# A streaming trunk layer: input-projection blocks in another order, decay matrices masked on VectorE in pairs, and head norms joined 120 matmuls later

## The chip, the cores and the metric

The kernel runs on one core of a Trainium2 chip. The time is device time in microseconds (us); the figure of a kernel is the median over its runs. TensorE (PE) multiplies matrices, VectorE (DVE), ScalarE (ACT) and GpSimd (POOL) do elementwise work, SyncE (SP) starts DMAs.

## The reference

One layer of a hybrid encoder for 256 prompt rows and 64 rows of a running stream, with one set of fp32 weights. A combined input projection feeds two groups of channels: 8 convolution groups (gate, causal convolution of width 31, group norm, swish) and 8 heads of a gated delta rule. Then come one output projection and a feed-forward network. Cut to what matters here:

```python
h = rmsnorm(x, g_pre_mix)
p = h @ w_in            # columns: conv values, conv gates, q, k, v, z, beta and decay inputs
# convolution groups
u = h_val * sigmoid(h_gate)
u = causal_dwconv(u, buf, w_dw, b_dw)              # 31 taps
a_out = silu(group_norm(u))
# heads
qkv = silu(causal_dwconv(qkv, buf, w_sc))          # 4 taps
G = cumsum(g)                                      # g: log decay of each row and head
decay = exp(where(incl, G[i] - G[j], -inf))        # lower triangle, for each head and chunk
m = where(strict, (k * beta) @ k.T * decay, 0);  tmat = inverse(m + eye)
o = ...                                            # chunked recurrence with tmat and decay
o = o * rsqrt(mean(o * o) + EPS) * onorm_g         # head norm
b_out = o * silu(z)
x = x + rmsnorm(concat(a_out, b_out) @ w_out, g_post_mix)
# feed-forward: w_up, convolution of width 3, silu(gate) * up, w_down
```

## The kernel before

All 320 rows are the moving side of each matmul, 128x320. A weight block of 128 output channels and 2048 inputs comes as two DMA halves of 128x1024. ScalarE rounds a half to `whi` (L182), VectorE subtracts to get the rest, `wlo` (L183), and a block takes 48 matmuls: for each of its 16 slices `whi` by the high part of the rows, `whi` by their low part (L198, L199), and `wlo` by the high part (L202). There are three buffers for a split half. These 48 are called dense matmuls below; the blocks follow each other on TensorE without any other order than the program's.

The input projection has 56 such blocks. `PLAN`, a list of steps, sets their order: `c0` is the gate block and the value block of convolution 0, `h0` the k, q and v blocks of head 0, `z0` the block of head 0's output gate, and `g` starts the decay matrices of all heads. `FIRST` names four blocks that are multiplied ahead of the list, while the rows are still being split; `in_block` hands them out of `ready` when the list comes to them.

The work that is not dense is written as jobs, Python generators. After each 20 dense matmuls (`GAP`) the jobs that are due are moved on by one step, and a `yield` with a number of matmuls (`LAG_...`) says how much later the next step may be issued. A step issues a few small matmuls and the elementwise work behind them. As each engine runs its instructions in order, a small matmul whose input is late holds up all dense matmuls behind it. The jobs that matter here:

- `gates`: from `baT` (L378) through the log decay `gt` (L412) to six small matmuls into `psg` (L423), exponentials on ScalarE, and then five rounds: VectorE spreads the decays (`rg`, L441), TensorE sums them (`psd`, L444), ScalarE takes the exponential (`eg`, L445), GpSimd multiplies by a triangle of ones and stores the piece of a head's decay matrix `E` (L448).
- `conv_block` and `conv_tail`: after the value block come one tap on ScalarE (L473) and 30 taps on VectorE (`cvt`, L475). 400 matmuls later (`LAG_CONV`) TensorE transposes the result (`pt_c`, L484), and the group norm follows, from `bst` (L486) to `un` (L495).
- `gdn_tail` and `pair`: two heads make a pair. Its triangular inverse is found by levels of small matmuls (`pz`, `px`, `py`, L685 to L693, joined on VectorE in `wtp`, L694 and L695), then the recurrence runs (`vn`, `po`, L740 and L742). The head norm scales the result `ot` on ScalarE (L805), and after `LAG_NORM` matmuls TensorE transposes it (`pt_o`, L814).

ScalarE holds one set of function tables at a time; where a function of another set follows, the program has an `ACT_TABLE_LOAD` of its own ahead of it.

## Time and profile before

| what | value |
|---|---|
| median of 3 runs | 1543.32 us (1542.33 to 1543.33) |
| the profiled execution's own time | 1543.88 us |
| its span in the trace | 1542.1 us |
| TensorE busy | 1513.1 us, 98% of the span |
| VectorE, ScalarE, GpSimd busy | 1006.5, 728.3 and 332.5 us |
| TensorE idle in the stretch from 40 to 560 us | 18.1 us |

The profiled execution is one run, 0.56 us above the median; some 1.8 us of it lie outside the span. Busy time of TensorE counts a matmul from its start to its modelled end, also where the clock is low, so that a slow stretch is hidden in it.

### The profile page before, as it was taken

What the parts mean: (1) busy time and instruction counts of PE and PEld (TensorE: products, weight loads), DVE (VectorE), ACT (ScalarE), POOL (GpSimd) and SP (SyncE); (2) the same over time, 40 slices, a digit from 0 to 9 for tenths busy, and PEclk for the clock granted to TensorE, in tenths of its full rate; (3) what the DMA queues carried; (4) which work ended last, traced back from release to release, by engine and by line L of the source; (5) the groups of instructions that cost most, each with busy time, mean ns of one, the idle gap of its engine ahead of it and who ended that gap; (6) DMA issues with size and microseconds to landing.
All of it is one profiled execution on the core that took longest, in us unless ns stands there. A gap on an engine that the chain in (4) does not pass through costs nothing.

```text
span 1542.1 us, 26538 instructions
## 1 busy us (share of the span) xinstructions
PE 1513.1 (98%) x10249; PEld 1489.1 (97%) x10249; DVE 1006.5 (65%) x1828; ACT 728.3 (47%) x1203; POOL 332.5 (22%) x501
## 2 busy tenths in 40 slices
PE   9989999989999999999999999999999999999998
PEld 8979999989899998899999999999999999999997
DVE  6789969586898468756534666545566545566554
ACT  7655464545545465544434444433444333444453
POOL 0354424153211000323101222101222101232101
PEclk9999999999999999999999999999999999999999
DMA  8434444353444563344445444445444345444443
GB/s 295 143 95 145 126 122 142 105 153 113 109 132 127 154 232 113 115 153 145 132 150 167 148 151 150 129 151 172 151 151 151 127 150 168 153 147 153 131 150 115
DMA packets 95991, 224.31 MB, mean 145 GB/s; under 512 B 18424, under 2 KB 37112, under 8 KB 95736
## 3 DMA queue, kind: packets, MB, share of 16 engines
q1 hardware_dynamic: 95720, 222.57, 46.4%
q8 instruction: 81, 1.33, 0.4%
q14 instruction: 46, 0.38, 0.1%
q10 hardware_dynamic: 144, 0.03, 0.0%
HBM read 215.45 MB, written 7.12 MB: 144 GB/s over the span
## 4 chain that ended last, share of the span: by engine, by line
PE 80%; DVE 12%; POOL 3%; ACT 2%; issue 2%; DMA 1%; SPq 0%; DVEq 0%; ACTq 0%; POOLq 0%
PE psu L202 13%; PE psu L198 13%; PE psu L199 13%; PE psdn L198 7%; PE psdn L199 7%; PE psdn L202 7%; DVE wlo L183 4%; DVE cvt L475 3%; PE psq L202 2%; PE psq L198 2%; PE psq L199 2%; PE psm L202 1%; PE psm L198 1%; PE psm L199 1%; PE ps_first L352 1%
## 5 line engine op out<-in xcount | busy, mean ns | idle before, releaser
L182 ACT CAST whi<-w 128x1024 fp32r<-128x1024 f32 (+2 forms) x432 | 411.3, 954 | 516.7 <-PE psu L199 170.7
L183 DVE TENSOR_TENSOR wlo<-w,whi 128x1024 fp32r<-128x1024 f32 (+2 forms) x432 | 477.1, 1105 | 198.1 <-ACT whi L182 111.4
L198 PE MATMUL psu<-hi,whi 128*128 128x320 f32 x1344 | 397.5, 309 | 2.9 <-DVE fbuf L1014 2.9
L199 PE MATMUL psu<-lo,whi 128*128 128x320 f32 x1344 | 397.5, 309 | 0.0
L198 PEld LDWEIGHTS psu<-hi,whi 128*128 128x128 f32 x1344 | 252.6, 188 | 3.4 <-DVE fbuf L1014 3.4
L199 PEld LDWEIGHTS psu<-lo,whi 128*128 128x128 f32 x1344 | 252.7, 188 | 0.0
L1015 POOL COPY nffn<-fbuf 128x2 f32<-128x2 f32 x88 | 101.4, 1152 | 599.5 <-DVE fbuf L1013 598.9
L202 PE MATMUL psu<-hi,wlo 128*128 128x320 f32 x1344 | 225.5, 310 | 0.0
L199 PE MATMUL psdn<-gl,whi 128*128 128x320 f32 x704 | 208.9, 309 | 0.0
L198 PE MATMUL psdn<-gh,whi 128*128 128x320 f32 x704 | 208.8, 310 | 0.0
L202 PEld LDWEIGHTS psu<-hi,wlo 128*128 128x128 f32 x1344 | 204.9, 189 | 0.0
L1013 DVE TENSOR_TENSOR fbuf<-psu,rb 128x256 f32<-128x256 f32 x88 | 37.4, 425 | 177.3 <-PE psu L202 174.8
L475 DVE SCALAR_TENSOR_TENSOR cvt<-ub,par,cvt 128x350 f32<-128x350 f32 x240 | 139.8, 596 | 2.7 <-ACT cvt L473 0.2
L198 PEld LDWEIGHTS psdn<-gh,whi 128*128 128x128 f32 x704 | 132.1, 188 | 0.8 <-ACT gh L206 0.8
L199 PEld LDWEIGHTS psdn<-gl,whi 128*128 128x128 f32 x704 | 132.1, 188 | 0.3
L202 PE MATMUL psdn<-gh,wlo 128*128 128x320 f32 x704 | 124.0, 309 | 0.0
L202 PEld LDWEIGHTS psdn<-gh,wlo 128*128 128x128 f32 x704 | 108.5, 188 | 0.0
L198 PE MATMUL psq<-hh,whi 128*128 128x320 f32 x352 | 106.1, 315 | 0.8 <-DVE baT L379 0.8
L199 PE MATMUL psq<-hl,whi 128*128 128x320 f32 x352 | 104.9, 311 | 0.0
L198 PEld LDWEIGHTS psq<-hh,whi 128*128 128x128 f32 x352 | 66.9, 190 | 1.1 <-ACT whi L182 1.0
L199 PEld LDWEIGHTS psq<-hl,whi 128*128 128x128 f32 x352 | 66.9, 190 | 0.0
L1057 DVE TENSOR_TENSOR y<-y,psdn 128x320 f32<-128x320 f32 x48 | 23.4, 488 | 63.9 <-PE psdn L202 63.9
(314 smaller groups left out, 2369.1 us busy)
## 6 DMA issues: line engine op xcount, KB each, us to landing
w<-in_w_up SPq DMA_DIRECT2D x176, 512.0 KB, 3.6
w<-in_w_in SPq DMA_DIRECT2D x88, 512.0 KB, 3.5
w<-in_w_down SPq DMA_DIRECT2D x64, 384.0 KB, 3.0
w<-in_w_down SPq DMA_DIRECT2D x64, 320.0 KB, 2.7
w<-in_w_out SPq DMA_DIRECT2D x32, 384.0 KB, 3.1
w<-in_w_out SPq DMA_DIRECT2D x8, 512.0 KB, 3.7
w<-in_w_first SPq DMA_DIRECT2D x6, 512.0 KB, 5.4
wtp<-wsp SPq DMA_DIRECT2D x4, 640.0 KB, 5.2
```

Of the source, the lines that this page charges most:

```text
L182: S.copy(hi[:, 0:width], w[:, 0:width])
L183: V.tensor_tensor(lo[:, 0:width], w[:, 0:width], hi[:, 0:width].bitcast(F32), ALU.subtract)
L198: tick(PE.matmul(ps, wh, xh, start=(k0 + j == 0), stop=False))
L199: tick(PE.matmul(ps, wh, xl, start=False, stop=False))
L202: tick(PE.matmul(ps, lo[:, j * P:(j + 1) * P], xh, start=False, stop=(final and k0 + j == nk - 1)))
L352: tick(PE.matmul(ps, w, xh, start=(k == 0 and wt is hi), stop=(k == KB - 1 and wt is lo)))
L475: V.scalar_tensor_tensor(cvt, ub[:, t:t + 350], pv("w_dw", b * 31 + t), cvt, ALU.mult, ALU.add)
L1013: V.tensor_tensor(buf[:, 2:258], psu[:, 0:TP], rb2[:, 0:TP], ALU.mult)
L1015: G.tensor_copy(nffn[:, b, 0, :], buf[:, 256:258])
L1057: V.tensor_tensor(y[:, n, :], y[:, n, :], psd[:, 0:T], ALU.add)
```

## The change

Five edits, in the order of the code:

- `FIRST` names the output-gate blocks of heads 0 and 1 (40 and 41) in place of the gate and value block of convolution 0. `PLAN` begins with them, starts `g` next, and then alternates heads and convolutions.
- `LAG_NORM` goes from 60 to 120.
- The decay matrices of two heads share one tile, `E2`. The triangle is multiplied on VectorE, for two heads in one instruction, 12 in all, in place of 24 on GpSimd. Tiles of the output projection and the feed-forward network that used the old buffers take halves of the new ones.
- A convolution that stands two before in the list is finished between the gate block and the value block of a `conv_block`, and no longer ahead of both.
- At heads 2, 4 and 6 the first block of the head is multiplied ahead of what was forced there, and the pair before the last is moved on only until its head norm is scaled (`free`), and no longer finished.

```diff
-LAG_NORM = 60
+LAG_NORM = 120
-PLAN = "c0 g h0 h1 c1 z0 c2 z1 h2 h3 z2 z3 c3 h4 h5 c4 z4 h6 h7 c5 z5 c6 z6 z7 c7"
+PLAN = "z0 z1 g h0 h1 c0 z2 h2 c1 h3 z3 c2 h4 c3 z4 h5 c4 h6 c5 z5 h7 c6 z6 z7 c7"
-FIRST = (8, 0, 24, 16)
+FIRST = (40, 41, 24, 16)
     def split_mix(i, x):
-        b_hi[i] = act.tile([P, T], F32R, tag=f"bh{i}", name=f"bh{i}")
+        if i < 8:
+            b_hi[i] = act.tile([P, T], F32R, tag=f"bh{i}", name=f"bh{i}")
+        elif i % 2 == 0:
+            both = act.tile([P, 2, T], F32R, tag=f"bp{i // 2 - 4}", name=f"bp{i // 2 - 4}")
+            b_hi[i:i + 2] = both[:, 0, :], both[:, 1, :]
...
-        E = [act.tile([P, T], F32, tag=f"bh{8 + h}", name=f"E{h}") for h in range(NH)]
+        E2 = [act.tile([P, 2, T], F32, tag=f"bp{i}", name=f"E{i}") for i in range(NH // 2)]
+        E = [E2[h // 2][:, h % 2, :] for h in range(NH)]
...
             S.activation(eg, psd, AF.Exp)
-            for j in range(w):
-                m = cv("tri") if c < 2 else cv("tri2")[:, (j % 2) * n:(j % 2 + 1) * n]
-                G.tensor_tensor(E[h0 + j][:, c * P:c * P + n], eg[:, j * n:(j + 1) * n], m, ALU.mult)
+            for j in range(w // 2):
+                if c < 2:
+                    m = cv("tri").unsqueeze(1).to_broadcast((P, 2, n))
+                else:
+                    m = cv("tri2").rearrange("p (b i) -> p b i", b=2)
+                V.tensor_tensor(E2[h0 // 2 + j][:, :, c * P:c * P + n],
+                                eg[:, 2 * j * n:2 * (j + 1) * n].rearrange("p (b i) -> p b i", b=2), m, ALU.mult)
...
         psv = in_block(b, "psv")
+        if b > 1:
+            finish(convs[b - 2])
...
             S.activation(ot[:, a, :], ot[:, a, :], AF.Identity, scale=t1[:, a:a + 1])
+        st["free"] = True
         yield LAG_NORM, 0, 2
...
     def z_block(h):
-        psz = ps_p.tile([P, 512], F32, tag="p", name="psz")
-        block_matmul(psz[:, 0:T], ins["w_in"][40 + h], hx, (8, 8))
+        psz = in_block(40 + h, "psz")
...
         if kind == "c":
-            if i > 1:
-                finish(convs[i - 2])
             convs[i] = start(conv_tail(i, conv_block(i)), LAG_CONV, 0, 1)
...
             if i % NS == 0:
-                if i // NS > 1:
-                    finish(pairs[i // NS - 2])
+                if i:
+                    ready[24 + i] = in_block(24 + i, "psq")
+                while i // NS > 1 and "free" not in sts[i // NS - 2]:
+                    advance(pairs[i // NS - 2])
                 st = {}
+                sts.append(st)
                 pairs[i // NS] = start(pair(i // NS, st), 0)
```

How the change moves instructions, at three places. The first is ScalarE in the stretch where the decay matrices are made. Before, one table load (L426, for the exponentials) stands there, the five `eg` follow it, and the next load belongs to the sigmoid of an output gate, `zT`:

```order
L463 ACT_TABLE_LOAD
L463 ACTIVATE sg<-sg 128x320
L182 CAST whi<-w 128x1024
L426 ACT_TABLE_LOAD
L426 ACTIVATE eG<-psg 128x24
...
L445 ACTIVATE eg<-psd 128x512 x2
L182 CAST whi<-w 128x1024
L445 ACTIVATE eg<-psd 128x512
L473 ACTIVATE cvt<-ub_589,par 128x350
L827 ACT_TABLE_LOAD
```

After, on ScalarE from the second `eg` of the five on, with the short convolution's `vts` and the gate `sg` of convolution 0 between them:

```order
L550 ACT_TABLE_LOAD
L550 ACTIVATE vts<-cq 128x64
L450 ACT_TABLE_LOAD
L450 ACTIVATE eg<-psd 128x512
L182 CAST whi<-w 128x1024
L472 ACT_TABLE_LOAD
L472 ACTIVATE sg<-sg 128x320
L182 CAST whi<-w 128x1024
L450 ACT_TABLE_LOAD
L450 ACTIVATE eg<-psd 128x512
```

The exponentials have moved in among other functions, so that tables are loaded between them; the whole program has 22 such loads before and 29 after.

The second place is VectorE where the first convolution is joined. Before, the last taps of convolution 0 (input `ub_588`) alternate with those of convolution 1 (`ub_589`), right in front of the group norm's `BN_STATS`, which reads what TensorE has transposed:

```order
L475 SCALAR_TENSOR_TENSOR cvt<-ub_588,par,cvt 128x350
L475 SCALAR_TENSOR_TENSOR cvt<-ub_589,par,cvt 128x350
L475 SCALAR_TENSOR_TENSOR cvt<-ub_588,par,cvt 128x350
L589 TENSOR_SCALAR tq_1279<-ssq_598 128x2
L475 SCALAR_TENSOR_TENSOR cvt<-ub_589,par,cvt 128x350
L590 TENSOR_SCALAR tq_1279<-ssq_598 128x2
L475 SCALAR_TENSOR_TENSOR cvt<-ub_589,par,cvt 128x350
L486 BN_STATS bst<-pt_c 128x6 x2
```

After, on VectorE, the last tap of convolution 0 (line numbers have moved by 11), then what is left of a pair's inverse, 14 taps of convolution 1 and splits of weights (cut here), and the join:

```order
L658 TENSOR_TENSOR tmp<-wi,dn 40x72
L486 SCALAR_TENSOR_TENSOR cvt<-ub_588,par,cvt 128x350
L471 TENSOR_TENSOR sg<-psgate,rb 128x320
L660 TENSOR_REDUCE wi<-tmp 40x2x6
L183 TENSOR_TENSOR wlo<-w,whi 128x1024
...
L486 SCALAR_TENSOR_TENSOR cvt<-ub_589,par,cvt 128x350
L548 SCALAR_TENSOR_TENSOR cq<-qb_594,par,cq 128x323
L183 TENSOR_TENSOR wlo<-w,whi 128x1024
L497 BN_STATS bst<-pt_c 128x6 x2
```

The taps of one convolution no longer alternate with the next one's, and 41 rows stand between the last of them and the group norm, 8 of them `wlo`. Counted so for convolutions 0 to 7, VectorE has 0, 5, 1, 6, 4, 0, 8 and 13 `wlo` between the last tap and the join before, and 8, 7, 5, 8, 3, 6, 6 and 11 after.

The third place is TensorE between the recurrence of heads 2 and 3 (pair 1) and the transposes of their norm. Before, the last `po`, one block's first 40 dense matmuls (cut here), `pt_o`:

```order
L740 MATMUL po<-vn,kd 128x128 x2
L742 MATMUL po<-vn,at 128x128 x2
L198 MATMUL psq<-hh_90,whi 128x320
...
L199 MATMUL psq<-hl_121,whi 128x320
L814 MATMUL pt_o<-cst,ot 128x128 x6
L202 MATMUL psq<-hh_98,wlo 128x320
```

After, on TensorE, with 120 dense matmuls between the two:

```order
L751 MATMUL po<-vn,kd 128x128 x2
L753 MATMUL po<-vn,at 128x128 x2
L202 MATMUL psgate<-hh_94,wlo 128x320
...
L202 MATMUL psq<-hh_101,wlo 128x320
L826 MATMUL pt_o<-cst,ot 128x128 x6
L202 MATMUL psq<-hh_102,wlo 128x320
```

For pairs 0 to 3 the numbers of dense matmuls between the last `po` and `pt_o` are 60, 40, 60 and 80 before, and 120 for each after. From the second part of the output projection on, VectorE, ScalarE and GpSimd have the same instructions in the same order as before.

## Rows read from the trace of the kernel before

**Rows 1.** Page, part 1: busy us (share of the span) and instructions by engine.

```profile
PE 1513.1 (98%) x10249; PEld 1489.1 (97%) x10249; DVE 1006.5 (65%) x1828; ACT 728.3 (47%) x1203; POOL 332.5 (22%) x501
```

**Rows 2.** Stretches: length, busy us of each engine, granted clock, DMA share, GB/s.

```profile
40.00:560.00 520.00, 501.89 (x3442) 491.64 (x3441) 409.79 (x840) 273.34 (x574) 154.94 (x224) 0.98 0.44 134
560.00:1542.00 982.00, 972.54 (x6564) 961.67 (x6563) 570.19 (x951) 427.51 (x588) 174.07 (x269) 1.00 0.47 145
```

**Rows 3.** What TensorE waited for: us in total, times, longest us.

```profile
PE pt_o L814 <- ACT ot L805: 7.3, 2, 4.2
PE pt_c L484 <- DVE cvt L475: 4.7, 2, 4.2
...
PE pz L685 <- DVE wtp L695: 2.1, 1, 2.1
...
PE psq L198 <- DVE baT L379: 0.8, 1, 0.8
PE psg L423 <- DVE gt L412: 0.7, 1, 0.7
```

**Rows 4.** Stretches before 560 us with a granted clock of 0.50; columns as in Rows 2.

```profile
84.10:87.40 3.30, 3.30 (x9) 2.27 (x9) 2.36 (x4) 0.60 (x1) 1.86 (x3) 0.50 0.44 127
108.00:111.30 3.30, 2.92 (x12) 2.92 (x13) 2.68 (x13) 0.27 (x2) 2.52 (x6) 0.50 0.21 86
268.40:275.10 6.70, 6.70 (x28) 6.70 (x28) 6.02 (x12) 1.79 (x4) 0.19 (x1) 0.50 0.34 86
319.60:322.90 3.30, 2.64 (x11) 2.64 (x12) 1.67 (x5) 2.46 (x6) 0.00 (x0) 0.50 0.47 156
415.20:418.50 3.30, 3.02 (x13) 3.03 (x14) 2.11 (x3) 2.10 (x3) 0.86 (x1) 0.50 0.00 0
```

**Rows 5.** Timeline of TensorE around the norms of pairs 1 and 2: start, us.

```profile
309.53 0.61 PE L742 MATMUL po<-vn,at 128*128 128x128 f32 x4
...
320.26 1.54 PE L814 MATMUL pt_o<-cst,ot 128*128 128x128 f32 x6 [4.25 <-ACT ot L805]
...
403.06 0.61 PE L742 MATMUL po<-vn,at 128*128 128x128 f32 x4
...
415.48 1.54 PE L814 MATMUL pt_o<-cst,ot 128*128 128x128 f32 x6 [3.01 <-ACT ot L805]
```

**Rows 6.** Timeline of TensorE in a dense stretch: eight matmuls, and the one behind them.

```profile
42.54 1.34 PE L202 MATMUL psq<-hh,wlo 128*128 128x320 f32 x8
43.72 0.31 PE L198 MATMUL psq<-hh,whi 128*128 128x320 f32 x1
```

**Rows 7.** Timeline of VectorE at the first convolution's join and in pair 1's levels.

```profile
105.77 2.55 DVE L475 SCALAR_TENSOR_TENSOR cvt<-ub,par,cvt 128x350 f32<-128x350 f32 x5
...
263.13 3.67 DVE L475 SCALAR_TENSOR_TENSOR cvt<-ub,par,cvt 128x350 f32<-128x350 f32 x6
```

**Rows 8.** Groups by line, 34 to 560 us: busy, mean ns; idle before, releaser.

```profile
L183 DVE TENSOR_TENSOR wlo<-w,whi 128x1024 fp32r<-128x1024 f32 (+1 forms) x123 | 142.9, 1162 | 54.4 <-ACT whi L182 31.6 <-PE psm L202 12.5 <-PE psq L202 4.1
...
L182 ACT CAST whi<-w 128x1024 fp32r<-128x1024 f32 (+1 forms) x124 | 122.8, 994 | 83.4 <-PE psm L199 27.9 <-PE psq L199 19.4 <-PE psgate L199 10.9
...
L448 POOL TENSOR_TENSOR E<-eg,cst 128x128 f32<-128x128 f32 (+1 forms) x24 | 15.4, 672 | 4.3 <-ACT eg L445 4.3
```

**Rows 9.** Timeline of VectorE, two of the five spreads of the decays.

```profile
85.72 0.69 DVE L441 TENSOR_TENSOR rg<-cst,gt 128x512 f32<-128x512 f32 x1 [0.91 <-PE psd L444]
...
91.11 0.95 DVE L441 TENSOR_TENSOR rg<-cst,gt 128x512 f32<-128x512 f32 x1
```

**Rows 10.** Timeline of ScalarE around a table load, and at one `eg`.

```profile
59.11 0.24 ACT L539 ACTIVATE vts<-cq 128x64 f32<-128x64 f32 x1
59.36 1.28 ACT L389 ACT_TABLE_LOAD   x1
60.66 0.22 ACT L389 ACTIVATE beta<-ba 128x24 f32<-128x24 f32 x1
...
88.78 0.60 ACT L445 ACTIVATE eg<-psd 128x512 f32<-128x512 f32 x1 [2.47 <-POOL E L448]
```

More of the change, by code (lines that the diff above doesn't have):

```diff
@@ L840, in trunk_kernel @@
     plan = PLAN.split()
-    tails, convs, pairs = {}, {}, {}
+    tails, convs, pairs, sts = {}, {}, {}, []
     for step in plan:
@@ L1028, in trunk_kernel @@
     for q in range(NQ):
-        gh = [act.tile([P, T], F32R, tag=f"bh{j}", name=f"gh{j}") for j in range(QB)]
+        gh = [act.tile([P, T], F32R, tag=f"bh{j}", name=f"gh{j}") for j in range(8)]
+        for i in range(2):
+            both = act.tile([P, 2, T], F32R, tag=f"bp{i}", name=f"gp{i}")
+            gh += [both[:, 0, :], both[:, 1, :]]
         gl = [act.tile([P, T], F32R, tag=f"bl{j}", name=f"gl{j}") for j in range(QB)]
```

## The prediction, made before the result was known

> **What bounds the kernel now.** I read the page's first part before anything else. TensorE is busy for 98% of the span, VectorE for 65%, ScalarE for 47% and GpSimd for 22% [rows 1]. The change adds no dense matmul and takes none away, so it can win only what TensorE loses, and it can lose wherever TensorE begins to wait. The next view is the two stretches: from 40 to 560 us (input projection and the first part of the output projection) TensorE is busy 501.89 of 520.00 us, and behind it 972.54 of 982.00 [rows 2]. The instructions of the second stretch are the same in both kernels, so only the 18.1 us of idle time in the first are in reach.
>
> The third view says what this idle time waited for: the transposes of two head norms 7.3 us, those of two convolutions 4.7, one level of an inverse 2.1, the gates' `baT` 0.8 and `gt` 0.7 [rows 3]. That is 15.6 us; 2.5 are left in small waits.
>
> The fourth view is the clock. Five stretches before 560 us show a granted clock of 0.50, the 1.2 GHz level in place of 2.4, with TensorE busy 18.58 us in all [rows 4]. At the full clock about half of that would do, so another 9.3 us are lost, which no list of waits shows. Four of the five stretches lie where TensorE had just stood still for 2 to 4 us (the norms at 320.26 and 415.48 [rows 5], the first convolution's join, the level). The fifth, at 84 us, follows the short wait for `gt` and six small matmuls. Waits and clock together make 27.4 us, which is the most that this change can win.
>
> A rule for the cost of a moved join: a dense matmul starts 0.147 us after the one before (eight from 42.54 to 43.72 [rows 6]), so 120 of them cover 17.7 us, 60 cover 8.8.
>
> **The change, part by part.**
>
> *Head norms.* Pair 1's last `po` starts at 309.53 and `pt_o` could start at 320.26: 10.7 us. Pair 2's chain takes from 403.06 to 415.48, 12.4 us [rows 5]. With 40 and 60 matmuls ahead they were 4.25 and 3.01 us late. After the change each pair has 120, 17.7 us, so both have some 5 us to spare, and no input of the chain is moved behind it. I take away the 7.3 us and half of the slow stretches that follow (2.64 and 3.02 us busy, 2.8 us): −10.1.
>
> *Convolution joins.* The stall of 4.2 us came where the last taps of convolution 0 alternate with those of convolution 1: five taps end at 108.32 [rows 7], and TensorE starts there. The other of the two, 0.5 us, was convolution 5's join. These are the joins with no split of weights between last tap and group norm (0 of both 0 and 5 in the counts by convolution). In the new order the least count is 3 and six of eight have 6 or more. TensorE needs each split within a half block's 24 matmuls, 3.5 us, so a tap that stands ahead of three splits which TensorE must have read before the join ends some 5 us or more before it. I take away 4.7 us and half of 2.92: −6.2. The bound: nothing gained, where VectorE runs late as a whole.
>
> *Pair 1's level.* Six taps in a row, 3.67 us from 263.13, stood ahead of `wtp` [rows 7]; TensorE waited 2.1 us and then ran 6.70 us at the lower clock. In the new order no `wtp` of this pair stands behind more than one tap. −2.1 − 3.35 = −5.5.
>
> *The gates.* The output gates of heads 0 and 1 stand ahead of them in place of convolution 0. One more VectorE operation stands ahead of `baT`, worth some 0.4 us, so that I take 1.2 in place of 0.8; the chain to `gt` meets about the same matmuls, and I take 1.0 in place of 0.7 and 0.3 for the first `psd`. The low clock at this place I leave as it is. Small waits grow from 2.5 to 3.1, since there are as many joins as before. Together +1.6; from −1.5, if all these go, to +4.
>
> *Masks.* 24 multiplications leave GpSimd, 15.4 us [rows 8], and 12 come to VectorE. The trace shows no such instruction. The nearest is the spread `rg` of 512 columns, 0.69 us with GpSimd idle and 0.95 beside the masks [rows 9]; half its columns is about 0.35 us, a quarter 0.2: eight and four of them make 3.6 us. Bounds are 0 (if what VectorE gets back from an idle GpSimd is as much: 0.26 us for each of several operations) and 12 × 0.95 = 11.4. VectorE is busy 409.79 of 520.00 us [rows 2], 79%, so 3.6 us more find room; TensorE pays only where a join is late, which the joins above carry. 0.
>
> *Table loads.* 7 more, 1.28 us each [rows 10], are 9.0 us on ScalarE, most of them among the five `eg`. In this stretch of some 21.5 us of dense matmuls I count for ScalarE 7 loads 9.0, 7 `whi` of 0.99 [rows 8] 7.0, five `eg` of 0.6 [rows 10] and, estimated, as much in small ones, less what overlaps, 5.5: 21.5 us. So it is just full there, with three buffers of split weights ahead. I take 0, since a load is issued ahead of its data, in time in which ScalarE waited (83.4 us ahead of `whi` in the whole stretch [rows 8]). The other end is 9.0, all of it.
>
> The trace shows the function ahead ending at 59.35, the load starting at 59.36 and ending at 60.64, and the next function starting at 60.66 [rows 10]: nothing drains on either side of it. The Trainium skill, page "ScalarE: Activation LUTs", section "What ACT_TABLE_LOAD costs", puts a switch at a 1283 ns load and a drain of about 1380 ns, 2.66 us together. The trace agrees with the load and shows no drain; by the page seven loads would be 18.6 us, and if all of it came to TensorE the forecast would lose its whole gain.
>
> *The other edits* add no instruction. A convolution's tail, forced between gate and value block, and a pair, forced behind the k block, get 48 dense matmuls more ahead of them, 7.1 us of cover; the pair is forced only as far as its scaled norm. Weight loads keep number and size and follow the order of the blocks on SP's queue, with DMA busy 44% [rows 2]; no split waits for them longer than before as long as that queue runs three buffers ahead. 0; without that cover they are the late joins that come next.
>
> *What comes late instead.* In the new VectorE order four taps stand right ahead of a `wtp` of pair 3, two thirds of the stack that cost pair 1 its stall; and the last convolutions' tails are forced just ahead of the output projection. I have walked the order, not the time, so I put in one new late join of the size of the level: 2.1 us and 1.5 of low clock, +3.6; bounds 0 and three of them, 10.8.
>
> The sum: −10.1 − 6.2 − 5.5 + 1.6 + 3.6 = −16.6. The profiled execution took 1543.9, which gives 1527.3; the median of the runs is 0.56 lower, so that 1526.7, **1527 us**, is the prediction. With the bounds of the likeliest case (gates −1.5 to +4, new joins 0 to 10.8) it lies between 1520 and 1536.
>
> **The rivals.**
>
> *ScalarE becomes the bound while the decay matrices are made.* For it: the count above leaves nothing over, and the first split that is late stops TensorE for each load that follows. Against it: the buffers ahead, and before, ScalarE waited 2.47 us ahead of an `eg` for GpSimd's masks [rows 10], which now are gone. All loads on the path cost 9.0 us, and a stall there is followed by the low clock that is there already: 1526.7 + 9.0 = 1535.7.
>
> *Only the head norms gain.* Their gain rests on a distance; the two others on where VectorE's work happens to stand, and a stall can move to the next join. For it: VectorE is 79% busy, and each stall that goes lets TensorE ask for splits sooner. Against it: the counts of splits. −10.1 alone, with 0 for all others: 1533.2.
>
> *Nothing measurable.* The gain is eaten by both: loads 9.0 and two late joins at 3.6 more. 1526.7 + 16.2 = 1542.9.
>
> *Slower: convolution joins late as a rule.* The one mechanism is that a `conv_block` now comes after each head, so that its 30 taps (17 us by [rows 7], 0.51 each) share VectorE with a head's taps, the inverse and the masks. If VectorE does not get through them within the 400 matmuls (59 us), each join stops TensorE as the one at 108 did, 4.2 us and 1.5 of low clock, 5.7. Without any late join the change gains 10.1 + 6.2 + 5.5 − 1.6 = 20.2; four late joins cost 22.8 and make it even, within what a measurement can tell, five make it slower by 8, and all eight give 1543.3 + 45.6 − 20.2 = 1568.7. For it: the share of VectorE. Against it: before, pairs of convolutions shared it at the same time and two joins of eight were late.
>
> **How the numbers follow.** 0.2% of the time, 3.1 us, is about what a measurement of this kernel can tell from no change. Chances: the forecast 0.60, ScalarE the bound 0.13, only the norms 0.13, nothing measurable 0.08, slower 0.06. The first three are all faster, 0.86. The likeliest case's own bounds are 1520 to 1536. The range goes below it by the small waits that might go too, to 1518, and up over both lesser gains to 1540; what lies outside is the last two cases, 0.14, and a little below.
>
> **What would show it.** In the trace after: no wait of `pt_o` on `ot` over 0.5 us, and 120 matmuls between; no `pt_c` behind `cvt`; no low clock at these places; `baT` and `gt` still waited for, about 1 us each, with a low clock behind them; TensorE idle about 10 us in the first 560 us; masks of about 0.35 us on VectorE; no `whi` waited for while the `eg` are made. The prediction is wrong if `psgate`, `psq` or `psz` wait for `whi` between two `eg` (ScalarE), if `pt_c` waits three times or more (VectorE), or if a low clock stands where nothing had stood still.

## The result, and the profile after

The changed kernel takes 1545.70 us (median of 11 runs, 1543.4 to 1548.98), the kernel before 1542.86 beside it (11 runs, 1541.03 to 1544.9). The ratio is 1.0022, 95% interval [1.0013, 1.0031]: slower by 0.2%, where 1527 had been forecast and 1518 was the lowest, 1540 the highest time thought likely. The profiled execution, 1543.40 us with a span of 1541.6, is the fastest of the eleven.

One sentence ahead of the prediction was wrong, and the prediction took it over: the tail of the convolution two before is not forced between gate and value block, but behind the value block's matmuls. The waiting step has 96 dense matmuls more ahead of it, not 48.

The page's first part, after:

```profile
PE 1510.6 (98%) x10249; PEld 1487.3 (96%) x10249; DVE 1013.6 (66%) x1840; ACT 735.9 (48%) x1210; POOL 303.6 (20%) x477
```

VectorE has 7 us more and GpSimd 29 us less than in [rows 1]; TensorE is as full as it was. The stretches that answer to [rows 2], after, with the stretch of the gates:

```profile
40.00:560.00 520.00, 499.65 (x3437) 490.37 (x3437) 415.62 (x852) 279.86 (x579) 126.13 (x200) 0.98 0.45 134
560.00:1542.00 982.00, 972.25 (x6573) 961.41 (x6571) 571.51 (x952) 428.61 (x590) 173.99 (x269) 1.00 0.48 146
...
80.00:100.00 20.00, 20.00 (x128) 18.51 (x128) 14.62 (x27) 13.35 (x16) 0.86 (x1) 1.00 0.46 134
```

TensorE is idle 20.35 us in the first stretch, 2.2 more than before. The forecast had left 10.8 us for idle time and low clock together (27.4 less 16.6); they are 28.0. While the decay matrices are made (the five `psd` start at 73.6 to 98.0 us) TensorE has no idle time at all: 20.00 us of 20.00 in the last row, and 29.00 of 29.00 from 72 to 101 us. What it waited for, after, to be read beside [rows 3]:

```profile
PE pz L696 <- DVE wtp L706: 4.7, 1, 4.7
PE pt_o L826 <- ACT un L506: 4.0, 2, 3.5
PE psm L198 <- DVE ub L480: 4.0, 1, 4.0
...
PE px L701 <- ACT zs L697: 2.3, 1, 2.3
PE po L751 <- ACT vn L745: 1.8, 1, 1.8
...
PE psq L198 <- DVE baT L383: 1.2, 1, 1.2
...
PE psv L202 <- DVE wlo L183: 0.9, 1, 0.9
PE pks L624 <- ACT vh L616: 0.8, 1, 0.8
PE psg L428 <- DVE gt L416: 0.3, 1, 0.3
```

The reader is to see that no wait of [rows 3] is left but the two of the gates: no `pt_o` waits for `ot`, no `pt_c` for `cvt`, and the `pz` of the first line has the names of one in [rows 3] but belongs to another pair (pair 2, at 367 us, where it had been pair 1). In their place stand the seven lines that are not of the gates, 18.5 us; before, TensorE waited at none of these places for more than 0.6 us. The clock, after, at the places where it is low:

```profile
84.10:87.40 3.30, 3.30 (x20) 2.82 (x20) 1.28 (x2) 2.67 (x4) 0.86 (x1) 1.00 0.55 159
163.90:167.20 3.30, 3.30 (x14) 3.30 (x14) 3.30 (x10) 0.56 (x2) 1.40 (x3) 0.51 0.19 77
232.00:235.30 3.30, 3.30 (x13) 3.30 (x14) 3.30 (x8) 0.81 (x2) 1.71 (x2) 0.50 1.01 271
365.50:371.10 5.60, 3.38 (x15) 3.41 (x16) 5.60 (x12) 0.43 (x1) 0.00 (x0) 0.50 0.45 127
447.00:453.60 6.60, 5.28 (x20) 5.31 (x21) 5.46 (x12) 1.86 (x3) 0.00 (x0) 0.50 0.76 221
```

The stretch at 84 us, low in [rows 4], now has the full clock. The four low ones lie at the four longest of the new waits, TensorE busy 15.3 us in them, half of which, 7.6, is lost.

**Three of the new waits, read in the timeline.** VectorE ahead of the level of pair 2, after:

```profile
360.23 3.05 DVE L486 SCALAR_TENSOR_TENSOR cvt<-ub,par,cvt 128x350 f32<-128x350 f32 x6
363.18 0.49 DVE L837 TENSOR_TENSOR zT<-psz,rb 128x320 f32<-128x320 f32 x1
363.59 1.22 DVE L183 TENSOR_TENSOR wlo<-w,whi 128x1024 fp32r<-128x1024 f32 x1
364.72 2.06 DVE L486 SCALAR_TENSOR_TENSOR cvt<-ub,par,cvt 128x350 f32<-128x350 f32 x4
366.69 0.48 DVE L705 TENSOR_TENSOR wtp<-wtp,px 128x320 f32<-128x320 f32 x1
367.09 0.49 DVE L706 TENSOR_TENSOR wtp<-wtp,py 128x320 f32<-128x320 f32 x1
```

Ten taps, a split and an output gate stand ahead of the sums that the next `pz` reads at 367.72. In the program's order, where the taps of two convolutions take turns, each of them is a row of its own. TensorE at the norm of pair 0, after:

```profile
209.55 0.61 PE L753 MATMUL po<-vn,at 128*128 128x128 f32 x4
...
221.74 0.49 PE L495 MATMUL pt_c<-cst,cvt 128*128 128x128 f32 x3
...
227.93 0.49 PE L826 MATMUL pt_o<-cst,ot 128*128 128x128 f32 x3
...
231.95 0.89 PE L826 MATMUL pt_o<-cst,ot 128*128 128x128 f32 x3 [3.53 <-ACT un L506]
```

The norm itself is in time (the first `pt_o` waits for nothing, 18 us behind `po`). Those of the second head need a buffer of PSUM, the memory that TensorE writes its results to. The pool for transposes has two, and convolution 1's transposes, 40 dense matmuls ahead, hold one until their group norm has read it. ScalarE ahead of pair 0's recurrence, after:

```profile
192.52 1.28 ACT L472 ACT_TABLE_LOAD   x1
193.82 0.47 ACT L472 ACTIVATE sg<-sg 128x320 f32<-128x320 f32 x1
194.19 0.35 ACT L745 ACTIVATE vn<-pvn,sc 128x128 f32<-128x128 f32 x1
194.56 1.28 ACT L512 ACT_TABLE_LOAD   x1
195.86 0.62 ACT L512 ACTIVATE af<-pt_c,par 128x320 f32<-128x320 f32 x1
196.37 0.36 ACT L745 ACTIVATE vn<-pvn,sc 128x128 f32<-128x128 f32 x1
```

Two table loads stand ahead of the second `vn`, for which TensorE waits 1.8 us.

### The profile page after: what moved, and what is told of

It reads as the page before. It is cut to its first block, busy times and chain, and to the rows that moved or that the text cites. A ratio compares the mean times of both kernels' runs of the same rounds, so it can differ in the third digit from the quotient of the medians.

```text
span 1541.6 us, 26524 instructions
## 1 busy us (share of the span) xinstructions
PE 1510.6 (98%) x10249; PEld 1487.3 (96%) x10249; DVE 1013.6 (66%) x1840; ACT 735.9 (48%) x1210; POOL 303.6 (20%) x477
## 4 chain that ended last, share of the span: by engine, by line
PE 83%; DVE 9%; ACT 3%; POOL 2%; issue 2%; DMA 0%; DVEq 0%; ACTq 0%; POOLq 0%
PE psu L198 13%; PE psu L199 13%; PE psu L202 13%; PE psdn L198 7%; PE psdn L199 7%; PE psdn L202 7%; DVE wlo L183 3%; DVE cvt L486 3%; PE psm L202 2%; PE psm L198 2%; PE psm L199 2%; PE psq L202 2%; PE psq L198 2%; PE psq L199 2%; PE ps_first L356 1%
## 5 line engine op out<-in xcount | busy, mean ns | idle before, releaser
L198 PE MATMUL psdn<-gh,whi 128*128 128x320 f32 x512 | 152.3, 309 | 0.0
L198 PEld LDWEIGHTS psdn<-gh,whi 128*128 128x128 f32 x512 | 96.1, 188 | 0.0
L202 PE MATMUL psdn<-gh,wlo 128*128 128x320 f32 x512 | 95.8, 309 | 0.0
L202 PEld LDWEIGHTS psdn<-gh,wlo 128*128 128x128 f32 x512 | 80.4, 188 | 0.0
```

Source lines behind the costliest of these rows:

```text
L198: tick(PE.matmul(ps, wh, xh, start=(k0 + j == 0), stop=False))
L202: tick(PE.matmul(ps, lo[:, j * P:(j + 1) * P], xh, start=False, stop=(final and k0 + j == nk - 1)))
```

## The experiments

Theories: **A**, the forecast gains are real and the new order of blocks makes other joins late; **B**, masks on VectorE and table loads on ScalarE overload these; **C**, the longer distance itself costs; **D**, for one run, the new order is as good as the old one by itself; **E**, came up after the first four: a wait that is taken away comes back at another join. All runs in one table; *before* is the kernel before in runs beside them on the same chip, *idle* is TensorE's between 40 and 560 us in the one profiled execution, *clock* the mean granted clock over the runs.

| run | median us | before | ratio, 95% | idle us | clock |
|---|---|---|---|---|---|
| changed kernel | 1545.70 | 1542.86 | 1.0013 to 1.0031 | 20.4 | 0.992 |
| e1_norm60 | 1545.06 | 1542.60 | 1.0005 to 1.0023 | 19.1 | 0.992 |
| e2_masks_pool | 1547.41 | 1542.60 | 1.0020 to 1.0043 | 22.3 | 0.992 |
| e3_old_order | 1546.48 | 1542.60 | 1.0016 to 1.0036 | 19.2 | 0.991 |
| e4_before_norm | 1539.80 | 1542.60 | 0.9977 to 0.9996 | 17.7 | 0.993 |
| e5_before_plan | 1545.29 | 1542.73 | 1.0012 to 1.0031 | 22.1 | 0.993 |
| e6_pst3 | 1548.16 | 1542.73 | 1.0020 to 1.0045 | 18.9 | 0.991 |
| e7_norm140 | 1546.52 | 1542.73 | 1.0017 to 1.0039 | 21.0 | 0.992 |
| e8_level30 | 1539.43 | 1542.73 | 0.9976 to 0.9994 | 16.9 | 0.994 |
| g1_taps20_after | 1541.38 | 1543.18 | 0.9979 to 0.9997 | 19.1 | 0.994 |
| g2_taps20_before | 1540.56 | 1543.18 | 0.9973 to 0.9992 | 20.9 | 0.993 |
| g3_norm_level30 | 1541.10 | 1543.18 | 0.9976 to 0.9993 | 16.2 | 0.992 |
| g4_old_finish | 1542.49 | 1543.18 | 0.9987 to 1.0005 | 19.4 | 0.993 |
| h1_old_order_masks | 1550.08 | 1543.12 | 1.0031 to 1.0059 | 20.0 | 0.988 |
| h2_level30_old_finish | 1541.64 | 1543.12 | 0.9982 to 1.0000 | 17.6 | 0.992 |
| h3_norm_taps20 | 1536.17 | 1543.12 | 0.9942 to 0.9971 | 14.4 | 0.994 |
| h4_norm_first_step | 1552.97 | 1543.12 | 1.0051 to 1.0075 | 22.7 | 0.989 |
| i1_level30_old_first | 1542.46 | 1542.66 | 0.9990 to 1.0008 | 17.8 | 0.994 |
| i3_level30_both | 1534.70 | 1542.66 | 0.9937 to 0.9962 | 15.9 | 0.996 |

In each of the 20 profiled executions, span less idle time less what the clock took, (1 − clock) × span, comes to 1508.6 to 1512.8 us. So, to within some 4 us, waits and clock are what differs between the kernels, and no dense matmul was added or taken away in any of them. A difference of 2 or 3 us between two kernels lies inside what this account leaves open.

**One part at a time.** Distance back to 60 in the changed kernel:

```diff
-LAG_NORM = 120
+LAG_NORM = 60
```

> The changed kernel with LAG_NORM back at 60; all else of the change stays. Theory A (stalls have moved: the 120 takes away the waits of pt_o on ot as worked out, and what is lost comes from joins that the new order of the blocks makes late): the one wait of pt_o for a PSUM buffer (3.5 us and 1.65 of low clock at 232 us) goes, but with 60 matmuls, 8.8 us, ahead, at least the norms of pairs 1 and 2 (chains of 10.7 and 12.4 us before) wait on ot again, some 2 and 3.6 us with 1.5 of low clock behind each: 1546 to 1551, not faster than the changed kernel. Theory C (the distance itself is what costs): at least 3 us faster than the changed kernel, 1542 or less.

1545.06, not told apart from the changed kernel: C falls. But the sum of A was wrong in detail: no `pt_o` waits for `ot` here either; one waits 4.5 us for a buffer that `kd` reads, and two `px` 3.8 us for `zs`. So in the new order, with the new rule at the heads, it is not the distance of 120 that keeps the head norms from being late: at 60, pair 0's `pt_o` starts 9.3 us behind its last `po` (219.75 and 210.49 us) and finds its input there.

The masks on GpSimd again, with the old loop over single heads:

```diff
-                V.tensor_tensor(E2[h0 // 2 + j][:, :, c * P:c * P + n],
...
+                G.tensor_tensor(E[h0 + j][:, c * P:c * P + n], eg[:, j * n:(j + 1) * n], m, ALU.mult)
```

> The changed kernel with the 24 masks on GpSimd again, written into the same pair tiles. Theory A: masks cost nothing in either place, 1543 to 1549, as the changed kernel, and the stretch where the decay matrices are made is no faster. Theory B (VectorE and ScalarE are overloaded: masks and table loads make the other joins late): 1540 or less, with fewer waits of pz, px and po.

1547.41, within the intervals the same: in this order the place of the masks does not matter, and B falls for the masks. The table loads, the other half of B, are 29 in this run too; no run in this order takes them away.

The old order with all else of the change:

```diff
-PLAN = "z0 z1 g h0 h1 c0 z2 h2 c1 h3 z3 c2 h4 c3 z4 h5 c4 h6 c5 z5 h7 c6 z6 z7 c7"
+PLAN = "c0 g h0 h1 c1 z0 c2 z1 h2 h3 z2 z3 c3 h4 h5 c4 z4 h6 h7 c5 z5 c6 z6 z7 c7"
-FIRST = (40, 41, 24, 16)
+FIRST = (8, 0, 24, 16)
```

> The changed kernel with the old FIRST and PLAN; distance, masks, and the rules of what is forced stay. Theory A: the waits of pt_o on ot (10.1 us with clock) are gone, those of the old order (first convolution's join, a level of pair 1, gt) are back: 1543 - 10 = 1533, range 1529 to 1538. Theory B: 1543 or more, since masks are on VectorE here too. Theory C: 1543 or more.

1546.48, 13 us over A's number, which falls as stated: the order of blocks is not the one culprit.

Distance and heads' rule alone, in the kernel before:

```diff
-LAG_NORM = 60
+LAG_NORM = 120
...
+                if i:
+                    ready[24 + i] = in_block(24 + i, "psq")
+                while i // NS > 1 and "free" not in sts[i // NS - 2]:
+                    advance(pairs[i // NS - 2])
```

> The kernel before with LAG_NORM 120 and the new rule at heads 2, 4 and 6 (k block first, pair moved on only until its norm is scaled), since without it pair 1 is forced at 40. Order, masks and convolution rule as before. Theory A: 10.1 us less than before, 1533, range 1529 to 1538. Theory C (the distance is no gain): 1541 or more.

1539.80: faster, by 2.8 of the 10.1 us, and short of A's range. What TensorE waited for in this run:

```profile
PE pt_c L484 <- DVE cvt L475: 9.8, 2, 5.1
...
PE pz L685 <- DVE wtp L695: 2.9, 1, 2.9
PE px L690 <- ACT zs L686: 1.9, 1, 1.9
```

The 7.3 us of `pt_o` are gone, as worked out; convolution 5's join, 0.6 us late before, now is 5.1 us late, and `px` and `pz` add 2.7. The wait went, most of the time did not.

The new order alone, in the kernel before (`FIRST`, `PLAN` and `in_block` for the output gates):

> The kernel before with the new FIRST and PLAN alone; distance, masks on GpSimd and the rules of what is forced are as before. Theory A (the new order brings late joins of its own): with neither the gain nor the collision of the longer distance it loses what it makes late, 1545 or more. Theory D (not the order: the new rules and the distance eat the gain, the order by itself is as good as the old one): 1543 or less. Theory B (masks on VectorE): 1540 or less.

1545.29, 2.6 us over the kernel before: the order by itself costs, as A says, and D falls. In it, `pt_c` waits 8.4 us for `un` (6.1 at most), `pt_o` 3.9 for a buffer.

**One new wait at a time.** A third buffer for the transposes:

```diff
-    ps_t = ctx.enter_context(tc.tile_pool(name="ps_t", bufs=2, space=PSUM))
-    ps_g = ctx.enter_context(tc.tile_pool(name="ps_g", bufs=4, space=PSUM))
+    ps_t = ctx.enter_context(tc.tile_pool(name="ps_t", bufs=3, space=PSUM))
+    ps_g = ctx.enter_context(tc.tile_pool(name="ps_g", bufs=3, space=PSUM))
```

> The changed kernel with a third PSUM buffer for transposes and one less (3 of 4) for the other small products. Theory A: the waits of pt_o and pt_c on un (4.3 us in the trace of the changed kernel, and 1.65 of low clock behind the longest) go, 1540; the levels of an inverse, which hold three of the other buffers at once, may pay, up to the same amount. Theory E (a wait that is taken away comes back at a later join, whatever it is, because VectorE or ScalarE is behind by then): 1544 or more with other waits longer.

1548.16. `pt_o` waits no more for `un`; `px` waits 4.8 us in place of 2.3, 3.5 of it at 252 us, and a long low clock follows there. As `px` is written to the pool that gave up a buffer, this run alone can't tell that price from E.

The distance at 140:

> The changed kernel with LAG_NORM 140. The norm of pair 0 comes 60 instead of 40 dense matmuls behind the first transposes of convolution 1, 8.8 us instead of 5.9, and those hold their buffer for 9.6 us by the trace. Theory A: of the wait of 3.5 us some 0.6 is left and no low clock follows, 4.5 us less: 1541, range 1539 to 1543. Theory E: within 2 us of the changed kernel, 1544 to 1548, the time lost at another place.

1546.52. The wait did what A says, to the tenth; TensorE at the second `pt_o` of pair 0 in this run:

```profile
231.59 0.55 PE L826 MATMUL pt_o<-cst,ot 128*128 128x128 f32 x3 [0.60 <-ACT un L506]
```

But `px` at 252 us and a `pt_c` at 431 us, in time before, now wait 2.6 and 1.4 us. This run leaves the pools as they are, and with it both speak for E. Its profiled execution, at 1541.83, is 3.9 us faster than any of its other six.

Twice the distance behind a level's sums:

```diff
             V.tensor_tensor(halves(TT, w, 0)[:, 0:nt], halves(TT, w, 0)[:, 0:nt], py[:, 0:nt], ALU.add)
-            yield LAG_WAIT, 1, 0
+            yield 30, 1, 0
```

> The changed kernel with the two steps behind a level's sums (wtp) 40 dense matmuls apart instead of 20, so that the ten taps in front of them have 2.9 us more. Theory A: the wait of pz on wtp, 4.7 us, shrinks to 1.8, with half of the low clock behind it left; the norms move by 20 to 40 matmuls, that of pair 0 out of its collision too, 3.5 and 1.65: 1537 to 1541. Theory E: 1544 or more, with waits of the same sum at other joins.

1539.43, within A's range, 6.3 us under the changed kernel and the interval below 1. Waits of this run:

```profile
PE px L701 <- ACT zs L697: 6.7, 3, 2.8
PE pt_o L826 <- DVE zo L828: 4.4, 1, 4.4
...
PE pt_o L826 <- ACT un L506: 1.9, 1, 1.9
...
PE pz L696 <- DVE wtp L706: 0.5, 1, 0.5
```

`pz` from 4.7 to 0.5, `psm` and `vn` gone, `pt_o` behind `un` 2.1 less: 12 us of waits. 8.8 us came back, in `px` and in `pt_o` behind `zo`. Here the balance is a gain, and E's 1544 or more was wrong. In the old order the same edit, on top of e4, finds nothing to gain:

> The kernel before with LAG_NORM 120, the new rule at heads 2, 4 and 6, and 40 instead of 20 dense matmuls behind a level's sums. If distances are what can be bought without moving blocks: 2.9 us and 1.7 of low clock at pair 1's level less than the run without the last edit (1539.8): 1535 to 1537. Theory E: 1539 or more, with other joins later.

1541.10, not told apart from 1539.80: `pz` no longer waits, `px` waits 1.3 us more and `po` 1.0, idle time is 1.5 us less, and the clock takes 1.0 more over the runs.

Forcing the tails ahead of the gate block again:

```diff
+            if i > 1:
+                finish(convs[i - 2])
             convs[i] = start(conv_tail(i, conv_block(i)), LAG_CONV, 0, 1)
...
-        if b > 1:
-            finish(convs[b - 2])
```

> The changed kernel with a convolution's tail forced ahead of the gate block again. With the old order of blocks, the edits that were not tried singly (masks on VectorE, this rule) cost 6.7 us together. If the rule is what costs, also in the new order: 1541 or less. If it costs nothing here (the order of blocks does): 1544 to 1548.

1542.49, between the two forecasts and 3.2 us under the changed kernel: the new place of the rule costs, in this order. That is no rule: with the old order and the masks on VectorE (e3 with this edit) the old place is the slower one.

> The kernel before with the distance of 120, the new rule at the heads and the masks on VectorE; order of blocks and the forced convolution tails as before. It stands between two runs: without the masks 1539.8, with the new place of the forced tails too 1546.5. If the masks cost in this order: 1543 or more. If the place of the forced tails does: 1541 or less.

1550.08, where e3 with the new place has 1546.48 and e4 without the masks 1539.80. The forecast for the masks came true, and more: moving them, with the shared tiles that go with it, costs 10 us in this order, where in the new order the place of the masks alone (e2) made no difference that could be told. No run holds the masks and the tiles apart in the old order. Pair 0's level now waits 4.9 us (put down to `nqkv` on GpSimd), and the clock takes 18.3 us over the runs, 6.8 more than in e4.

**Is VectorE too full?** Ten of 30 taps left out, in three kernels:

```diff
-        for t in range(1, 31):
+        for t in range(1, 21):
```

> The changed kernel without 10 of the 30 taps on VectorE in each convolution (left out of the computation), 80 instructions of 0.5 us, 41 us of VectorE; same matmuls, same order of blocks. Theory E (the late joins hang on taps that stand ahead of short work in VectorE's queue, so that a wait which goes comes back at the next join): with a third of the taps gone, TensorE's idle time from 40 to 560 us falls from 20 to 10 or less and the low clock with it: 1532 or less. Theory A (places of the order: buffers, table loads on ScalarE): most waits stay, 1540 or more.

> The kernel before without 10 of the 30 taps on VectorE in each convolution (left out of the computation). Theory E: the waits at the first convolution's join and at pair 1's level go, those for the norms stay, since they come from distances that are too short: 1534 to 1538, so that the changed kernel with the same cut is now the faster one. Theory A: the same gain in both, 0 to 4 us, and the changed kernel with the same cut is not faster.

> The kernel before with the distance of 120 and the new rule at the heads, without 10 of the 30 taps on VectorE in each convolution (left out of the computation). With all taps the norms' 10.1 us became 2.8, and the joins of convolutions 0 and 5 wait 4.6 and 5.1 us for taps. If TensorE's stall at the norms was VectorE's time to get through its taps (given back at the next join for want of VectorE): those two waits go and the gain of the distance comes out whole, 1530 to 1533. If the joins are late for their places: 1537 or more.

1541.38, 1540.56 and 1536.17; the first two are as A says. Each kernel is faster than with all taps, by 4.3, 2.6 and 3.6 us, so that the taps cost something. But with 35 to 38 us less VectorE work in the first stretch, idle time falls by only 1.3 us in the changed kernel and rises by 2.8 in the kernel before: most of the late joins do not hang on how much VectorE has to do in all. Nor do these runs clear its queue where a join is late. `pz` of pair 2 still waits 4.6 us with a third of the taps gone, since other taps stand there, nine where there had been ten. VectorE ahead of it in g1:

```profile
355.21 3.06 DVE L486 SCALAR_TENSOR_TENSOR cvt<-ub,par,cvt 128x350 f32<-128x350 f32 x5
...
359.71 2.43 DVE L486 SCALAR_TENSOR_TENSOR cvt<-ub,par,cvt 128x350 f32<-128x350 f32 x4
362.06 0.48 DVE L705 TENSOR_TENSOR wtp<-wtp,px 128x320 f32<-128x320 f32 x1
```

The `psm` at 445 us likewise waits 3.5 us (4.0 with all taps), behind seven taps in both kernels. So E, as a matter of VectorE's time in all, falls; as a matter of the taps that stand right ahead of a join it was not tested. The distance is worth 4.4 us with fewer taps (1540.56 to 1536.17) and 2.8 with all; 1536.17 lies between the two forecasts of h3. There the joins wait for no tap, but for `un`:

```profile
PE pt_c L499 <- ACT un L495: 8.5, 2, 5.7
```

That is the second transposes. Where a tail is forced, they come sooner behind the first than the 120 matmuls they are given otherwise: at convolution 5, 32 dense matmuls (4.7 us) stand between the two, and from the first transposes to the end of `un` it is 10.8 us.

**Two steps at once.** Forcing only the first transposes, behind the value block, in the old order (e4 with this):

```diff
-            if i > 1:
-                finish(convs[i - 2])
...
+        if b > 1 and b - 2 not in begun:
+            advance(convs[b - 2])
```

> The kernel before with the distance of 120, the new rule at the heads, and a convolution's tail forced only to its first transposes, behind the value block of the convolution two later (96 dense matmuls or 14 us later than before); the second transposes come 120 matmuls behind. The waits of 4.6 and 5.1 us for taps at convolutions 0 and 5 should go with 1.65 of low clock each, from 1539.8 to 1528, range 1526 to 1532. If waits come back at whatever join is next: 1537 or more.

1552.97, the slowest of all, where 1528 had been forecast. Neither join waits for taps now, and five other waits between 1.5 and 4.2 us came in (`pks`, a `pz`, a split on ScalarE, `pt_c` behind `un`, a `psm`).

Both gains of the new order together (the edits of e8 and g4 in the changed kernel):

> The changed kernel with 40 dense matmuls behind a level's sums and with convolution tails forced ahead of the gate block; one alone took 6.3 us from the changed kernel, the other 3.2. If waits are each other's neighbours but not each other's cause, both gains add: 1535 to 1538. If what one takes away comes back at the next late join: 1539 to 1543.

1541.64: the gains did not add. Three forced second transposes wait for `un`, 11.6 us with a small one. That kernel, with only the first step forced:

```diff
-            if i > 1:
-                finish(convs[i - 2])
+            if i > 1 and i - 2 not in begun:
+                advance(convs[i - 2])
```

> The changed kernel with 40 dense matmuls behind a level's sums and a convolution's tail forced, ahead of the gate block two later, only to its first transposes; the second ones follow 120 matmuls behind. Against the run that forces both steps at once (1541.6, three waits of the second transposes for un, 3.5 to 4.2 us each, 11.3 in all, three low clocks behind them). If these waits are the price of forcing two steps at once and nothing else takes their place: 1525 to 1531. If waits come back at other joins: 1537 to 1541.

1542.46, the waits have come back elsewhere: these 11.6 us are gone, and `pt_o` waits 6.2 us for `un`, `px` 5.7 us for `zs`. And with 40 matmuls between all steps of a level:

```diff
             S.copy(halves(zs, w, 0), pz)
-            yield LAG_WAIT, 2, 0
+            yield 30, 2, 0
```

> The run above with 40 dense matmuls between all steps of a level, so that the products px come 5.9 us behind pz. The waits of px on zs (2.2 to 2.8 us at pairs 0 and 1 in most variants of the new order, with low clock behind them) should go: 5 us of waits and 3 to 6 of low clock less than the run above. If waits come back at other joins: within 2 us of the run above.

1534.70, 0.9950 [0.9937, 0.9962]: faster than both kernels, by 8.0 and 11.0 us. Its waits and its first stretch:

```profile
PE pt_o L827 <- DVE zo L829: 5.2, 2, 3.1
...
PE pz L697 <- DVE wtp L707: 2.6, 1, 2.6
PE po L752 <- ACT vn L746: 1.6, 1, 1.6
```

```profile
40.00:560.00 520.00, 504.08 (x3489) 494.77 (x3488) 423.46 (x863) 287.86 (x592) 123.23 (x200) 0.99 0.47 138
```

No `px` waits. Idle time is only 1.8 us less than in i1, since other waits came in; the clock takes 3.8 us less over the runs (0.996 for 0.9935). Together that is 5.6 of the 7.8 us between the two medians; the rest lies within the 4 us that the account leaves open.

## Why the prediction was wrong

*What bounds the kernel* was right: what moved is idle time and clock, the idle time between 40 and 560 us, and the account closes to some 4 us for all 20 kernels.

*Head norms*: right in outcome, and in mechanism for the old order (e4). No `pt_o` waits for `ot`, −7.3 us and the low clock behind; in the new order these waits are gone at a distance of 60 as well (e1), so that there the gain is not the distance's. What the term did not ask is who holds the two PSUM buffers where the transposes now land: +3.5 us at pair 0. Taken alone (e4) the term was worth 2.8, not 10.1.

*Convolution joins*: right. No `pt_c` waits for `cvt`. Two figures on the way were off without changing the sum: 30 taps of 0.51 us are 15.3 us, not 17, and the forced tails got 96 matmuls of cover, not 48.

*Pair 1's level*: right in outcome for pair 1, where no level waits, but not for the reason given. VectorE ahead of the two `wtp` of pair 1, after:

```profile
257.16 1.56 DVE L486 SCALAR_TENSOR_TENSOR cvt<-ub,par,cvt 128x350 f32<-128x350 f32 x3
258.64 0.47 DVE L705 TENSOR_TENSOR wtp<-wtp,px 128x320 f32<-128x320 f32 x1
...
262.45 2.31 DVE L486 SCALAR_TENSOR_TENSOR cvt<-ub,par,cvt 128x350 f32<-128x350 f32 x4
...
265.94 0.49 DVE L705 TENSOR_TENSOR wtp<-wtp,px 128x320 f32<-128x320 f32 x1
```

Three taps stand right ahead of the first, four and a split ahead of the second; they were short enough, which is luck. The sentence that no `wtp` of this pair stands behind more than one tap was read from rows of the order; two convolutions whose taps take turns make rows of one tap each, and at pair 2 ten of them are in front. 4.7 us.

*The gates*: better than the +1.6. `baT` waits 1.2 as said, `gt` 0.3 in place of 1.0, the first `psd` nothing, and the low clock at 84 us, 1.65, went.

*Masks*: right. Twelve take 4.0 us on VectorE (3.6 forecast), and all five `rg` take 0.69. The group by line, after:

```profile
L456 DVE TENSOR_TENSOR E<-eg,cst 128x256 f32<-128x256 f32 (+1 forms) x12 | 4.0, 375 | 1.6 <-ACT eg L450 1.6
```

*Table loads*: right where they were looked for. Between the five `eg`, ScalarE was in time (80 to 100 us, above). Two of the loads stand elsewhere, ahead of the `vn` that is 1.8 us late; what they are worth there no run shows.

*What comes late instead* is the step that failed. It was put at 3.6 us, bounds 0 to 10.8. Measured: 18.5 us in the seven lines of new waits and 7.6 of low clock, 26.1. With the gates' +1.6 replaced by −1.6, the sum −10.1 − 6.2 − 5.5 − 1.6 + 26.1 is +2.7. Small waits of before that are gone (2.2 us) make it +0.5 for the traces' first 560 us; the span of the one after is even 0.5 shorter, since [rows 4] leave out a low clock of before at 637 us which this execution does not have. The median, 2.8 above that of before, is some 2 us above the profiled execution, the fastest of its kernel. Over the runs the mean clock is the same in both kernels (0.9923 in the 11 runs after, 0.9923 in the 26 runs of the kernel before beside e1), so that the clock is not what the medians differ by.

The idle time had been treated as something that can be emptied one wait after another, with one new one as a margin. The 18 experiments show it otherwise: idle time stays between 14 and 23 us in all of them, in e4 with four waits over 1 us, in e8 with six. The places are not random. With the new order, `pz` of pair 2 waits 4.6 to 4.7 us in the changed kernel, e2, e6, e7 and g1, and `psm` 2.1 to 4.0 us in these and in e1; with the old order and the longer distance, convolution 5's `pt_c` waits 5.0 to 5.1 us in e4, g3 and h1. An order of blocks has weak joins of its own. Both `pz` and `psm` stand behind a stack of taps, ten and seven, in stretches where VectorE is busy for 98 and 99% of the time (19.67 of the 20 us from 350 to 370, 19.79 from 430 to 450), and with twice the distance behind a level's sums (e8) `pz` waits 0.5 us and `psm` not at all.

None of the three signs of being wrong that the prediction named showed up. The sign of being right that failed was the idle time, 20 us where about 10 was to be seen.

The rival that came nearest in time was *nothing measurable*, 0.08, and in sign *slower*, 0.06; the mechanism of neither was at work (loads between the `eg` cost nothing, no convolution's first transposes were late), so that their nearness is chance.

**What stays open.** Why a wait that is taken away mostly comes back is not settled. VectorE's work in all is at most a small part of the reason (g1, g2); taps that stand in one heap ahead of a join are the likely one at `pz` and `psm`, but no run moved them and nothing else. Each edit also gives VectorE and ScalarE another order of short work between the matmuls, so that a variant is never one change alone, and the parts don't add: masks and their tiles +10 in one order, masks −2 (not told from 0) in the other, the forced tails +3 and −4. Which of the two, new order on the engines or later joins reached sooner, makes the new waits was not tried apart; that would need the order held fixed.

## What to carry to other kernels

Where idle time is spread over many short joins, a forecast that removes named waits needs a term for the waits that take their place, of the size of the idle time that is there (here 14 to 23 us), unless the new place of each join is checked against every resource that it needs: its input, the queue of each engine in the chain, and the buffer that it is written to. Row counts of an order hide stacks of work that alternate between two streams. More distance gained most where all steps of a chain that had none to spare got it (i3 against i1, 7.8 us).

## What was not expected of the hardware

The clock's price for the same wait differs from execution to execution. All 20 kernels have one wait in common, in the feed-forward network, where the instructions no longer differ: `psu` waits 2.9 us for `fbuf` (3.1 in e6), at 635.47 us in the kernel before and at 636.53 after. What followed, before and after:

```profile
637.10:640.40 3.30, 3.30 (x14) 3.30 (x14) 3.30 (x9) 2.82 (x6) 2.04 (x3) 0.50 0.01 2
```

```profile
637.10:640.40 3.30, 3.30 (x24) 3.30 (x24) 3.30 (x10) 2.73 (x5) 1.88 (x3) 1.00 0.03 10
```

In 5 of the 20 profiled executions no low clock followed (after, e4, h1, h3, i3), in 12 some 3.4 us of it, up to 1.7 us lost, and in 3 (e6, g2, h2) some 6.8 us, which began within the wait. In the first stretch it can be more. At 252 us of e7, behind a wait of 2.6 us, and of e6, behind one of 3.5:

```profile
252.00:262.00 10.00, 8.90 (x66) 8.67 (x67) 9.96 (x20) 3.43 (x7) 0.44 (x2) 1.00 0.33 108
```

```profile
252.40:262.40 10.00, 9.78 (x42) 9.78 (x42) 8.56 (x19) 2.47 (x4) 0.23 (x1) 0.51 0.32 106
```

In the one no low clock followed, in the other 10 us of it, 5 us lost. In e8 a wait of 2.8 us at the same join had 10 us of low clock behind it too, in a profiled execution of 1544.78 us at a mean clock of 0.991, while most runs of that kernel took 1539 at 0.994 or 0.995. So a stall of 2 to 4 us cost itself and 0 to 5 us more here, and a profile's low clock is one draw from that. The forecast's half of 3.3 us behind each was within it.
